# Five projection tiles summed block by block instead of four, with a sixth pair of split weight halves and a fourth adaLN buffer

## The chip, the cores and the metric

The kernel is one launch on one core of one Trainium2 chip. The metric is the device time of that launch in microseconds, the median of several runs. TensorE (PE) does the matrix products, VectorE (DVE) and ScalarE (ACT) the element-wise work, GpSimd (POOL) some sums and the small DMAs, and SyncE (SP) issues the large loads.

## What is computed

The trunk has two layers, and each layer is FFN, token mixer, FFN. That gives six sub-layers, numbered 0 to 5 here. Sub-layer 1 is the even mixer (windowed attention beside an RG-LRU), sub-layer 4 the odd mixer (HGRN2). There are 288 token columns: one prompt of 256 tokens and eight sequences of four. The width is 1024, kept as eight blocks of 128 rows. Each sub-layer is wrapped in the same way:

```python
def _pre(x, c, g_pre, ada_w, ada_b):
    mod = jax.nn.silu(c) @ ada_w + ada_b
    shift, scale, gate = jnp.split(mod[:, None, :], 3, axis=-1)
    return _rms_norm(x, g_pre) * (1 + scale) + shift, gate

def _post(x, y, gate, g_post, res_w):
    return x + res_w * (1 + gate) * _rms_norm(y, g_post)

def _swiglu(h, w_in, w_out):
    g, u = jnp.split(h @ w_in, 2, axis=-1)
    return (jax.nn.silu(g) * u) @ w_out
```

`h` is what `_pre` returns; the mixers too begin with a projection of `h` and end with a projection to `y`.

## The kernel before, in words

**Products.** Everything is kept transposed, features on partitions and 288 tokens in a row. A weight block W times h is three products of rounded halves: W_hi·h_hi, W_lo·h_hi and W_hi·h_lo. One output tile (128 features) of an input projection is `pj`, 8 blocks of h by 3 products, 24 matmuls. The output projection makes eight tiles `y0` to `y7` of 24 matmuls or more.

**Weights.** A load of 1 MB brings the weights of two `pj` tiles into one of `RAW` = 2 buffers `raw`; for each tile ACT rounds 128x1024 of it to `whi`, and DVE subtracts to get `wlo`. There are `HL` = 5 pairs of such halves. `split_some` issues the next split between matmuls when a pair is free in the plan.

**Order.** PE and SP run in the order in which the Python code emits. For ACT, DVE and POOL the framework sets an order when the program is built; it does not change at run time, so an instruction that waits holds up all that follows it on its engine. A planner (`clk`, `until`, `fill`, `ada_pace`, `drive`, `side`) keeps estimated times of all engines and decides between which matmuls the side work is emitted.

**From y to the next h (a transition).** After the last `y` tile the sums of squares (`yms`, `xyms`) are formed on PE, DVE and ACT make from them the two normalisers, which PE spreads (`yivb`, `xivb`), and then DVE and ACT make h block by block: `h0` high half, `h0` low half, `h1` and so on. `proj_in` meets these blocks with several tiles at once:

```python
for k in range(NB):
    group(range(outer), k)   # per tile 2 products with h_hi, then one with h_lo
...
for j in range(outer, n):    # the other tiles, one at a time
    w = get_w()
```

This first stretch is called the block phase here. `outer` is `OUTER` = 4, and it takes one weight pair for each of its tiles.

**adaLN.** The `mod` of every sub-layer comes from twelve chunks `ada` (two groups: eight of shift and scale, four of the gate), 64 chunks of 1 MB after the first eight, through `AW` = 3 buffers `aw`; SP issues each load when PE has read the buffer. After a group ACT copies it (`asb`), PE transposes it (`adaT`), and DVE writes `mod`. The planner uses a chunk, whole or in halves, to fill an expected wait of PE (`until`, `fill`), and otherwise spreads them (`ada_pace`). Where no chunk is at hand it may put a short `warm` product.

**Even mixer, end.** Its 14 tiles feed the recurrence (tiles 0 to 3), rotary and attention (4 to 9) and a gelu gate (10 to 13, `gx`). Attention runs as side work in four parts; scores of the eight short sequences are `scs`, their softmax `sms`, transposes `pT` and `pTs2`, products `pv1`, `pv0`, `pvs`. The gelu is done in `gated()`, which the last tile and the softmax of the short sequences both call: the one that is emitted second does it, with two loads of an activation table and the split of the gated result (`m`).

**Odd mixer, end.** For each of four pairs of heads a tree of products (`lv`, `sn`) runs beside the projection, with DVE and POOL updating Q, K and `acc` between its levels. Then come `ktp`, `sm`, `o`, the sum of squares `oms`, a normalisation on DVE and ACT, and the halves `o` of the pair, of which the output projection's `y0` needs all eight, in order; `o6` and `o7` are the last pair's.

Of the kernel before, what the change touches and what calls it, by code (L numbers as in the profile page):

```python
# [27 lines left out]
EPS = 1e-6  # L28
NEG = -1e30
NSUB = 6  # L30
RAW, HL, AW = 2, 5, 3
OUTER, KO = 4, 8
EV = 7.0
CV = (0.5, 1.5)
WARM = (28, 10, 4, 8, 8)
# [14 lines left out]
def tile_trunk(ctx: ExitStack, tc: tile.TileContext, I: dict, O: dict):  # L50
    nc = tc.nc
# [98 lines left out]
    def aux_ps(name):  # L150
        return ps.tile([128, 512], F32, tag="ps", name=name, bufs=8)

# [1 line left out]
    cT = cp.tile([128, NB, 32], F32, name="cT")  # L154
    SY.dma_start(cT, I["cT"].rearrange("p (k m) -> p k m", k=NB))
    sm = cp.tile([128, N_SMALL], F32, name="sm")
# [81 lines left out]
    sc = cT  # L238
    act(sc, cT, AF.Silu)

# [1 line left out]
    sides = []  # L242

    def dma_eta(nbytes, free=0.0):
# [25 lines left out]
    def until(*aps, gap=GAP, step=None):  # L270
        while ready(*aps) > clk["t"] + gap and (step or ada_ready()):
            if ada_ready():
                (step or ada_next)()
                run_sides()
            elif ready(*aps) > clk["t"] + KEEP:
                warm(1)
            else:
                break
# [15 lines left out]
            ada_next()  # L294
        clk["t"] = max(clk["t"], t)

# [1 line left out]
    units = []  # L298
    for i in range(NSUB):
        if i % 3 != 1:  # L300
# [31 lines left out]
    def get_w(load=True):  # L332
        q = oldest[0] = wat[0]
        wat[0] += 1
        split_to(q)
        if load:
            load_to(q // 2 + RAW)
        return splits[q]
# [7 lines left out]
    def mm3(out, w, o, hk, first, last):  # L346
        wh, wl = w[0][:, o:o + 128], w[1][:, o:o + 128]
        T.matmul(out, lhsT=wh, rhs=hk[:, 0, :], start=first, stop=False)
        T.matmul(out, lhsT=wh, rhs=hk[:, 1, :], start=False, stop=False)
        T.matmul(out, lhsT=wl, rhs=hk[:, 0, :], start=False, stop=last)  # L350

    def proj_in(n, hk, done, first=None):
        outer = OUTER
        ws = [get_w(False) for _ in range(outer)]
        oldest[0] = wat[0] - outer if not first else 0
        rest[0] = SPARE
        pp = [aux_ps(f"pj{j}")[:, :NT] for j in range(outer)]

        def group(js, k):
            o = 128 * k  # L360
            until(hk[k], gap=GAP if k else GAPS[4], step=ada_half)
            for j in js:
                T.matmul(pp[j], lhsT=ws[j][0][:, o:o + 128], rhs=hk[k][:, 0, :], start=k == 0, stop=False)
                T.matmul(pp[j], lhsT=ws[j][1][:, o:o + 128], rhs=hk[k][:, 0, :], start=False, stop=False)
            if first:
                first.finish(k)
            for j in js:
                T.matmul(pp[j], lhsT=ws[j][0][:, o:o + 128], rhs=hk[k][:, 1, :], start=False, stop=k == NB - 1)

        for k in range(NB):  # L370
            if first:
                first(k)
            group(range(outer), k)
            yield
        for j in range(outer):
            done(j, pp[j])
        for j in range(outer, n):
            w = get_w()
            p = aux_ps(f"pj{j}")[:, :NT]
            until(*w)  # L380
            for k in range(NB):
                mm3(p, w, 128 * k, hk[k], k == 0, k == NB - 1)
                yield
            done(j, p)
# [18 lines left out]
        A.activation(hk[:, 0, :], src, AF.Copy)  # L403
        V.tensor_tensor(out=hk[:, 1, :], in0=src, in1=hk[:, 0, :].bitcast(F32), op=OP.subtract)

# [1 line left out]
    mods = {}  # L407
    chunks = [(i, c) for i in range(NSUB) for c in range(NCH)]
    aw = []
# [107 lines left out]
            run_sides()  # L517
        drain()

# [1 line left out]
    def table(f):  # L521
        act(small("tab", [128, 1]), eps, f)

# [344 lines left out]
            side(x_stats(da.last))  # L868
        return hk

# [1 line left out]
    def ffn(hk, first=None):  # L872
        g2 = []
        st = {}

        def done(j, p):
            if j % 2 == 0:
                s = tmp("fs")
                act(s, p, AF.Silu)
                st["s"] = s  # L880
            else:
                m = st["s"]
                V.tensor_tensor(out=m, in0=m, in1=p, op=OP.mult)
                t = dbl(f"mh{j}", F32R)
                split_x(m, t)
                g2.append(t)

        drive(proj_in(2 * FB, hk, done, first))
        table(AF.Abs_reciprocal_sqrt)
        return g2  # L890

# [1 line left out]
    sp8 = cp.tile([128, 4], F32, name="sp8")  # L893
    sp16 = cp.tile([128, 4], F32, name="sp16")

# [68 lines left out]
    def even_mixer(hk):  # L964
# [194 lines left out]
        def done(j, p):  # L1159
# [17 lines left out]
            else:  # L1177
                b = j - 10
                A.activation(gxd[b // 2][:, b % 2, :], p, AF.Copy)
                if b == 3:  # L1180
                    gated()

        drive(proj_in(14, hk, done))
        drain()
        table(AF.Abs_reciprocal_sqrt)
        return mix

# [1 line left out]
    lb = cp.tile([128, 8], F32, name="lb")  # L1189
    oml = cp.tile([128, 8], F32, name="oml")  # L1190

# [183 lines left out]
    def odd_mixer(hk):  # L1375
# [39 lines left out]
        def gated(q, g, out):  # L1415
# [4 lines left out]
            split_x(o, out)  # L1420

        drive(proj_in(32, hk, done))
        drain()
        table(AF.Abs_reciprocal_sqrt)
        return mix

# [1 line left out]
    hk = None  # L1428
    for i in range(NSUB):
        first = None  # L1430
        if i == 0:
            hk, first = pre_first()
# [5 lines left out]
        mixer = i % 3 == 1  # L1438
# [10 lines left out]
def _prepare(a):  # L1449
# [37 lines left out]
    order = np.concatenate([np.arange(1280, 1792), np.arange(512, 768), heads, np.arange(768, 1280)])  # L1487
# [30 lines left out]
    r["rgw"] = g.transpose(1, 0, 2).reshape(128, 1024)  # L1518
    r["s0"] = a["state_s_hgrn"][0].transpose(1, 2, 0, 3).reshape(8, 128, 1024)

    # constants that depend on shapes alone
    r["ident"] = np.eye(128, dtype=f32)
    pos = np.concatenate([np.arange(NPR), np.tile(2048 + np.arange(TS), NSQ)]).astype(f32)
    inv = (f32(500000.0) ** (-np.arange(0, 16, 2, dtype=f32) / f32(16))).astype(f32)
# [72 lines left out]
```

## Time and profile before

| | before |
|---|---|
| median of 3 runs | 1321.88 us (1320.97 to 1321.97) |
| span of the profiled execution | 1320.2 us |
| PE busy | 1273.2 us, 96% |
| DVE, ACT, POOL busy | 61%, 47%, 17% |
| PE matmuls `pj` (with whi and with wlo) | 726.0 us and 519.0 us (they overlap in the records) |
| moved by DMA | 263.47 MB, 200 GB/s on average |

Matmuls overlap in the records, so busy PE time can be longer than the work; what a matmul costs is read from how many start in a stretch. The granted clock is 1.00 at 2.4 GHz and 0.50 at 1.2 GHz.

### The profile page before, as it was taken

How to read it: one execution, taken by the hardware profiler on the slowest of the kernel's cores; microseconds unless marked ns; L12 is line 12 of the kernel's file. 1: busy time of each engine (PE TensorE's matmuls, PEld its weight loads, DVE VectorE, ACT ScalarE, POOL GpSimd, SP SyncE). 2: the span in 40 equal slices, each digit the busy share in tenths (PEclk: the TensorE clock that was granted, in tenths of full speed). 3: DMA queues.
4: the chain of work that ended last, by engine and by line, in shares of the span. 5: the costliest groups of instructions: out<-in, count | busy, mean ns of one | idle time of the engine just before them, and what ended most of it. 6: DMA issues, size and time to landing. Idle time of an engine off the chain costs nothing. (4 is left out here: it accounts for less than half of the span.)

```text
span 1320.2 us, 25119 instructions
## 1 busy us (share of the span) xinstructions
PE 1273.2 (96%) x10267; PEld 1175.4 (89%) x10267; DVE 803.9 (61%) x1559; ACT 622.3 (47%) x1081; POOL 225.3 (17%) x303
## 2 busy tenths in 40 slices
PE   9999999999988999999899999989999989999995
PEld 7999999877687999999799999978788989999995
DVE  7644445688667555455754445488788777555433
ACT  5534444456654444444544444453445655444441
POOL 0000003263034000011400001153343132000011
PEclk9999999999999999999999999999999999999998
DMA  9786557466527745443675555367544452544441
GB/s 365 262 316 247 200 223 251 166 265 253 201 89 287 286 164 173 174 161 119 242 285 196 191 193 190 124 251 291 222 156 149 137 187 72 205 171 160 159 160 37
DMA packets 39556, 263.47 MB, mean 200 GB/s; under 512 B 4932, under 2 KB 5764, under 8 KB 9360
## 3 DMA queue, kind: packets, MB, share of 16 engines
q1 hardware_dynamic: 35280, 249.09, 51.6%
q0 software_dynamic: 4160, 12.77, 3.0%
q8 instruction: 81, 1.33, 0.4%
q14 instruction: 35, 0.29, 0.1%
HBM read 254.69 MB, written 7.15 MB: 198 GB/s over the span
## 5 line engine op out<-in xcount | busy, mean ns | idle before, releaser
L93 PE MATMUL pj<-h,whi 128*128 128x288 f32 x3552 | 726.0, 299 | 11.1 <-DVE h L93 8.6
L93 PEld LDWEIGHTS pj<-h,whi 128*128 128x128 f32 x3552 | 570.7, 189 | 45.9 <-issue 22.1
L93 DVE TENSOR_TENSOR wlo<-raw,whi 128x1024 fp32r<-128x1024 f32 x326 | 400.3, 1238 | 290.2 <-ACT whi L93 289.8
L93 PE MATMUL pj<-h,wlo 128*128 128x288 f32 x1776 | 519.0, 295 | 0.5 <-DVE wlo L93 0.5
L93 ACT ACTIVATE whi<-raw 128x1024 fp32r<-128x1024 f32 x326 | 340.4, 1058 | 341.4 <-PE pj L93 152.7
L93 PEld LDWEIGHTS pj<-h,wlo 128*128 128x128 f32 x1776 | 336.1, 189 | 0.7 <-DVE wlo L93 0.7
L93 PE MATMUL y<-mh,whi 128*128 128x288 f32 x1408 | 280.9, 295 | 0.0
L93 PEld LDWEIGHTS y<-mh,whi 128*128 128x128 f32 x1408 | 225.9, 188 | 2.9 <-issue 2.5
L93 PE MATMUL y<-mh,wlo 128*128 128x288 f32 x704 | 207.9, 295 | 0.0
L93 POOL TENSOR_TENSOR yss<-yss,ysq 128x288 f32<-128x288 f32 x55 | 59.5, 1082 | 789.4 <-ACT ysq L93 788.1
L93 PEld LDWEIGHTS y<-mh,wlo 128*128 128x128 f32 x704 | 132.4, 188 | 0.0
L93 DVE TENSOR_TENSOR fs<-fs,pj 128x288 f32<-128x288 f32 x88 | 39.5, 453 | 98.2 <-PE pj L93 90.9
L93 PE MATMUL ada<-aw,cT 128*32 128x512 f32 (+1 forms) x656 | 67.8, 515 | 0.0
L93 ACT ACTIVATE mh<-fs 128x288 fp32r<-128x288 f32 x88 | 37.7, 433 | 59.5 <-DVE fs L93 59.5
L93 ACT ACTIVATE fs<-pj 128x288 f32<-128x288 f32 x88 | 34.8, 400 | 37.1 <-PE pj L93 37.0
L93 ACT ACTIVATE h<-hn,mod 128x256 fp32r<-128x256 f32 x48 | 24.4, 509 | 56.1 <-DVE hn L93 56.1
L93 POOL TENSOR_TENSOR yg<-yg,yivs 128x288 f32<-128x288 f32 x38 | 34.0, 905 | 91.5 <-ACT yivs L93 91.5
L93 DVE TENSOR_TENSOR mh<-fs,mh 128x288 fp32r<-128x288 f32 x88 | 39.5, 453 | 11.2 <-ACT mh L93 11.2
L93 ACT ACT_TABLE_LOAD x27 | 34.6, 1283 | 16.2 <-PE pj L93 9.5
L93 PE MATMUL y<-o,whi 128*128 128x288 f32 x192 | 40.0, 302 | 0.5 <-DVE o L93 0.5
L93 ACT ACTIVATE ysq<-y 128x288 f32<-128x288 f32 x42 | 17.0, 404 | 44.1 <-PE y L93 44.1
L93 PEld LDWEIGHTS y<-o,whi 128*128 128x128 f32 x192 | 31.7, 193 | 1.8 <-ACT o L93 0.8
(289 smaller groups left out, 1086.9 us busy)
## 6 DMA issues: line engine op xcount, KB each, us to landing
raw<-in_wf_in SPq DMA_DIRECT2D x88, 1024.0 KB, 4.9
aw<-in_w_ada SPq DMA_DIRECT2D x64, 1024.0 KB, 5.0
raw<-in_wf_out SPq DMA_DIRECT2D x44, 1024.0 KB, 4.9
raw<-in_wo_in SPq DMA_DIRECT2D x16, 1024.0 KB, 6.9
awf<-in_w_ada SPq DMA_DIRECT2D x8, 1024.0 KB, 9.2
raw<-in_we_in SPq DMA_DIRECT2D x7, 1024.0 KB, 6.9
raw<-in_we_out SPq DMA_DIRECT2D x4, 1024.0 KB, 7.8
S<-in_s POOLq DMA_DIRECT2D x16, 256.0 KB, 7.3
```

The costliest lines, as they stand in the source:

```text
L93: r = f(*args, **kw)
```

## The change

`HL` goes from 5 to 6, `AW` from 3 to 4 and `OUTER` from 4 to 5; the first sub-layer keeps four tiles in its block phase. The room comes from `dynamic_dma_scratch_size=2048`, which makes the scratch of POOL's DMAs smaller: 2,048 bytes a partition instead of 16,384 in the built program. Six comment lines are left out too, without effect.

```diff
-RAW, HL, AW = 2, 5, 3
-OUTER, KO = 4, 8
+RAW, HL, AW = 2, 6, 4
+OUTER, KO = 5, 8
...
     def proj_in(n, hk, done, first=None):
-        outer = OUTER
+        outer = 4 if first else OUTER
...
-    nc = _bacc.Bacc("TRN2", target_bir_lowering=False, num_devices=1)
+    nc = _bacc.Bacc("TRN2", target_bir_lowering=False, num_devices=1, dynamic_dma_scratch_size=2048)
```

The planner answers the new buffers with another order everywhere. The products are the same, and there are four `warm` products and two loads of an activation table fewer (27 to 25). From the end of the even mixer on the adaLN chunks run earlier. At the end of the even mixer eight chunks stand between the last `pj` and `y0` instead of three. In the four later transitions fewer chunks stand before the second h block: three instead of four after sub-layers 0, 2 and 3, none instead of one after sub-layer 4, where a following transpose `adaT` also stood. In the odd mixer one chunk is left of eleven, and none stands in its `y0`. On SP, nine adaLN loads now go ahead of the last four weight loads of the even mixer's output projection.

Three places show what moved. The first is ACT at the end of the even mixer, from the second softmax of the short sequences (`sms`) on; `gx` is the gelu, `m` the gated result, `pTs` the copy that releases `pv0`. Before:

```order
L93 ACTIVATE sms,den<-sms,mx 128x288
L93 ACTIVATE es<-es 128x1
L93 ACTIVATE o_3913<-pv_3562 128x128
L93 ACT_TABLE_LOAD
L93 ACTIVATE gx_3030<-gx_3030 128x2x288
L93 ACTIVATE o_3916<-pv_3562 128x128
L93 ACTIVATE pTs<-pT 128x512
L93 ACTIVATE gx_3031<-pj_3884 128x288
L93 ACTIVATE m_3948<-ob 128x288
L93 ACTIVATE gx_3031<-gx_3031 128x2x288
```

Now:

```order
L93 ACTIVATE sms,den<-sms,mx 128x288
L93 ACTIVATE es<-es 128x1
L93 ACT_TABLE_LOAD
L93 ACTIVATE gx_3034<-gx_3034 128x2x288
L93 ACTIVATE gx_3035<-gx_3035 128x2x288
L93 ACT_TABLE_LOAD
L93 ACTIVATE tab<-eps 128x1
L93 ACTIVATE m_3949<-ob 128x288
L93 ACTIVATE m_3955<-ob 128x288
L93 ACTIVATE m_3961<-ob 128x288
L93 ACTIVATE m_3967<-ob 128x288
L93 ACTIVATE pTs<-pT 128x512 x2
```

Both copies `pTs` for `pv0` now stand behind the whole gelu; before, the first stood ahead of `sms` and the second in the middle of the gelu. PE meanwhile has, after `scs`, one set of four `pT` and two chunks ahead of `pv0`.

The second is PE at the end of the odd mixer, around the last pair of heads (`pj_11749` is the last projection tile, `y_11826` is `y0`). Before, from the products `o` on, with projection matmuls on both sides of them:

```order
L93 MATMUL pj_11701<-h_9410,wlo 128x288
L93 MATMUL pj_11749<-h_9403,whi 128x288 x2
L93 MATMUL pj_11749<-h_9403,wlo 128x288
L93 MATMUL o<-acc,vt 128x128 x2
L93 MATMUL o<-acc,vt 128x32
L93 MATMUL o<-sel,Xs 128x32
L93 MATMUL o<-Q_10981,smid 128x128
L93 MATMUL o<-acc,vt 128x128 x2
L93 MATMUL o<-acc,vt 128x32
L93 MATMUL o<-sel,Xs 128x32
L93 MATMUL o<-Q_10981,smid 128x128
L93 MATMUL pj_11749<-h_9404,whi 128x288 x2
```

Before, further on, inside `y0` ahead of `o6`:

```order
L93 MATMUL y_11826<-o_11695,whi 128x288 x2
L93 MATMUL y_11826<-o_11695,wlo 128x288
L93 MATMUL ada_11851<-aw_8_10095,cT 32x512 x4
L93 MATMUL ada_11851<-aw_9_10263,cT 32x512 x4
L93 MATMUL ada_11851<-aw_10_10408,cT 32x512 x4
L93 MATMUL y_11826<-o_11748,whi 128x288 x2
```

Now, from the end of the last projection tile to `y0`:

```order
L93 MATMUL pj_11710<-h_9472,wlo 128x288
L93 MATMUL ktp<-ident,K_10804 128x128 x4
L93 MATMUL sm<-vt,kt 128x128 x4
L93 MATMUL o<-acc,vt 128x128 x2
L93 MATMUL o<-acc,vt 128x32
L93 MATMUL o<-sel,Xs 128x32
L93 MATMUL o<-Q_10805,smid 128x128
L93 MATMUL o<-acc,vt 128x128 x2
L93 MATMUL o<-acc,vt 128x32
L93 MATMUL o<-sel,Xs 128x32
L93 MATMUL oms<-osq,ones 128x288 x2
L93 MATMUL y_11840<-o_11288,whi 128x288 x2
```

The projection matmuls that stood between the steps of the last pair, 21 between `ktp` and `sm`, 6 between `o` and `oms` and 15 after `oms`, are done before it, and the three chunks in `y0` are gone.

The third is DVE at the first transition, after the last `y` of sub-layer 0 (`nt` is the first step of the normaliser). Before:

```order
L93 SCALAR_TENSOR_TENSOR ysq_2821<-y_2717,modG_144,x 128x256
L93 TENSOR_TENSOR yg_2712<-y_2717,modG_144 128x32
L93 TENSOR_TENSOR ysq_2821<-x,yg_2712 128x32
L93 TENSOR_TENSOR ysq_2822<-yg_2712 128x32
L93 SCALAR_TENSOR_TENSOR nt<-yms,yiv 128x72
```

Now:

```order
L93 SCALAR_TENSOR_TENSOR ysq_2836<-y_2695,modG_144,x 128x256
L93 TENSOR_TENSOR yg_2690<-y_2695,modG_144 128x32
L93 TENSOR_TENSOR ysq_2836<-x,yg_2690 128x32
L93 TENSOR_TENSOR ysq_2837<-yg_2690 128x32
L93 TENSOR_TENSOR wlo<-raw,whi 128x1024
L93 SCALAR_TENSOR_TENSOR nt<-yms,yiv 128x72
```

A weight split stands between the squares and the normaliser there; its `whi` stands on ACT just ahead of `yiv`.

## Rows read from the trace of the kernel before

**Rows 1.** The page: costliest groups (busy us, mean ns, idle before, its main releaser).

```profile
L93 PE MATMUL pj<-h,whi 128*128 128x288 f32 x3552 | 726.0, 299 | 11.1 <-DVE h L93 8.6
...
L93 DVE TENSOR_TENSOR wlo<-raw,whi 128x1024 fp32r<-128x1024 f32 x326 | 400.3, 1238 | 290.2 <-ACT whi L93 289.8
...
L93 ACT ACTIVATE whi<-raw 128x1024 fp32r<-128x1024 f32 x326 | 340.4, 1058 | 341.4 <-PE pj L93 152.7
```

**Rows 2.** Timeline of PE after sub-layer 0 (start us, us; idle before and releaser).

```profile
265.97 1.07 PE L93 MATMUL ada<-aw,cT 128*32 128x256 f32 x16
...
270.36 0.96 PE L93 MATMUL adaT<-sm,asb 128*128 128x18 f32 x8
...
273.72 0.93 PE L93 MATMUL pj<-h,whi 128*128 128x288 f32 x5 [1.26 <-DVE h L93]
```

**Rows 3.** Stretches: length, busy time of PE, PEld, DVE, ACT, POOL, PEclk, DMA.

```profile
357.50:360.00 2.50, 2.31 (x19) 2.10 (x19) 0.00 (x0) 0.16 (x2) 0.00 (x0) 0.61 1.01 426
360.00:365.00 5.00, 5.00 (x22) 5.00 (x23) 0.77 (x4) 0.77 (x4) 0.00 (x0) 0.51 0.97 405
365.00:370.00 5.00, 5.00 (x40) 5.00 (x39) 0.65 (x2) 2.44 (x5) 0.72 (x1) 1.00 0.02 7
...
637.50:641.50 4.00, 3.90 (x18) 3.90 (x19) 4.00 (x17) 2.27 (x8) 0.75 (x1) 0.57 0.98 410
...
872.40:874.00 1.60, 1.52 (x8) 1.52 (x9) 1.60 (x7) 0.82 (x3) 1.24 (x2) 0.67 0.97 410
...
1085.00:1092.00 7.00, 5.13 (x19) 4.29 (x19) 5.91 (x16) 2.08 (x7) 4.81 (x6) 0.51 0.00 1
```

**Rows 4.** Timeline of PE after sub-layer 4, in the block phase.

```profile
1097.29 0.93 PE L93 MATMUL pj<-h,whi 128*128 128x288 f32 x5 [1.24 <-DVE h L93]
```

**Rows 5.** Timeline of PE at the end of the even mixer.

```profile
342.31 0.41 PE L93 MATMUL scs<-kv,qs 64*128 64x32 f32 x2
...
355.13 0.43 PE L93 MATMUL pvs<-pTss,vt 32*64 32x128 f32 x2 [1.06 <-ACT pTss L93]
...
357.69 0.43 PE L93 MATMUL pvs<-pTss,vt 32*64 32x128 f32 x2 [0.62 <-ACT pTss L93]
```

**Rows 6.** Timeline of ACT at the end of the even mixer.

```profile
347.09 0.53 ACT L93 ACTIVATE sms<-sms,mx 128x288 f32<-128x288 f32 x1 [0.43 <-DVE mx L93]
...
347.99 1.28 ACT L93 ACT_TABLE_LOAD   x1
349.28 0.68 ACT L93 ACTIVATE gx<-gx 128x576 f32<-128x576 f32 x1
...
350.03 0.59 ACT L93 ACTIVATE pTs<-pT 128x512 f32<-128x512 f32 x1
...
353.74 0.76 ACT L93 ACTIVATE m<-ob 128x288 fp32r<-128x288 f32 x2
```

**Rows 7.** Timeline of all engines at the end of sub-layer 1.

```profile
385.14 1.06 ACT L93 ACTIVATE whi<-raw 128x1024 fp32r<-128x1024 f32 x1 [2.65 <-DMA raw<-in_wf_in]
...
388.16 0.33 PE L93 MATMUL yms<-yss,ones 128*32 128x72 f32 x8 [1.21 <-POOL yss L93]
...
389.33 0.33 PE L93 MATMUL yms<-ysq,ones 128*32 128x72 f32 x8 [0.83 <-ACT ysq L93]
...
391.18 0.46 PE L93 MATMUL xyms<-ysq,ones 128*32 128x72 f32 x16 [1.26 <-DVE ysq L93]
```

**Rows 8.** Timeline of DVE after sub-layer 1, between the normaliser and x.

```profile
399.79 0.82 DVE L93 SCALAR_TENSOR_TENSOR modG<-mod,gph 128x72 f32<-128x72 f32 x1
```

**Rows 9.** Timeline of PE in the odd mixer, and of its end.

```profile
931.86 0.51 PE L93 MATMUL oms<-osq,ones 128*128 128x288 f32 x1 [1.42 <-ACT osq L93]
...
1048.00 1.13 PE L93 MATMUL oms<-osq,ones 128*128 128x288 f32 x4
...
1057.03 0.40 PE L93 MATMUL y<-o,whi 128*128 128x288 f32 x1 [0.50 <-DVE o L93]
```

**Rows 10.** Ten stretches of 20 us from 860 us: their sum over the odd mixer.

```profile
sum 200.00, PE 194.23 PEld 165.86 DVE 163.09 ACT 97.08 POOL 76.26; mean PE 19.42 PEld 16.59 DVE 16.31 ACT 9.71 POOL 7.63
```

## The prediction

> **What bounds the kernel now.** I began with the page. TensorE (PE) runs almost without a break, so the time is its work plus its idle time plus what it loses where its clock is granted at the lower level. The other engines matter only where PE waits for them. The costliest group tells of the largest single cause: PE stands 11.1 us ahead of `pj` matmuls, 8.6 of it for DVE's half of `h` [rows 1]. That is the block phase, at which the change aims. Then I read the timeline of PE at each transition and at the end of both mixers, and the granted clock of those stretches. In the first later transition the reader sees where chunks hide PE's waits, that a chunk costs 1.0 us and an `adaT` 0.8 us from start to start, and that the last wait, 1.26 us, is for the low half of `h1` on DVE [rows 2]. From the next block on PE no longer waits, with four tiles already. So a fifth tile helps only by what it puts ahead of that wait: three matmuls of `h0` and two of `h1`. A matmul takes 0.13 us at the full clock (40 records in 5 us) and 0.23 at half (22 in 5 us) [rows 3]. **Five matmuls are 0.66 us a transition**, not the whole wait, and a chunk that leaves this place takes back 1.0.
>
> **The change part by part.** All terms are PE time, against the profiled span of 1320.2 us.
>
> *After sub-layer 0.* 0.66 us more of `pj`, 1.0 us less of chunks: +0.3. The new `wlo` ahead of `nt` takes 1.24 us on DVE, on the chain that ends in `h1`; its `whi` of 1.06 us on ACT lies beside it and ahead of `yiv`, which would have waited for the sums about half of that [rows 1]. Behind it wait `nt`, both normalisers, all of `h`, and PE. +1.6 in all, between +0.5 (the split slips into an idle stretch of DVE) and +2.
>
> *End of the even mixer.* Before, PE waited here 1.06 and 0.62 us [rows 5] and then ran at half clock: (1 - 0.61) x 2.5 + (1 - 0.51) x 5.0 = 3.4 us lost [rows 3]. Together 5.1 us, which eight chunks instead of three might remove. But `pv0` now waits for a `pTs` behind the whole gelu on ACT, and the gelu stands behind `sms`, which needs `scs`. From the end of `scs` (342.72) [rows 5] to the second `sms` were 4.4 us, through DVE [rows 6]. Then come `sms` and `es` 0.6, a table load 1.28, two `gx` of 0.6, a second load 1.28, `tab` 0.1, four `m` of 0.38, one `pTs` of 0.6: 11.0 us [rows 6]. PE has four `pT` and two chunks for that time, 2.6 us. The wait is 8.4 us if the 4.4 stand, and 7.1 if the one `wlo` of 1.24 us [rows 1] inside them finds room elsewhere; I take 7.5. A wait of that length will be followed by half clock, as the stretch of 0.51 after sub-layer 4 was [rows 3]; part of such a stretch passes within the wait, so between 0 and 3.4 us are lost, and I take 1.0. Sum: 7.5 + 1.0 - 5.1 = **+3.4**, between +2.0 and +6.7.
>
> The table loads in this sum are weighed on ACT's rows: the gelu starts 1.29 us after its load starts, so a load costs 1.28 and no more [rows 6]. The Trainium skill (page "ScalarE: Activation LUTs", section "What ACT_TABLE_LOAD costs") gives 2.66 us for each switch, the load of 1283 ns and a drain of 1380 ns. By it the two switches would add 2.8 us and the sum would end at 1330.4 instead of 1327.6; the row shows the load alone, so I use that.
>
> *Transition after sub-layer 1.* Before, ACT stood 2.65 us for a weight load, and the sums behind it made PE wait 1.21, 0.83 and 1.26 us [rows 7]. The new order has most of these splits earlier; the nine adaLN loads ahead on SP delay four weight loads, but these are due only for the last tiles of `y` and for the next sub-layer. I keep 0.4 of the 3.3: -2.9. `modG`, 0.82 us [rows 8], and the small `mod` beside it leave the chain: -1.0. Five tiles: -0.7, with as many chunks as before. **-4.6**, between -5 and -1, the latter if a load is late again.
>
> *After sub-layers 2 and 3.* One chunk and the `adaT` leave, 1.8 us, and 0.7 comes: +1.1 each. Against it the half clock inside their block phases goes: (1 - 0.57) x 4.0 = 1.7 after sub-layer 2, and (1 - 0.67) x 1.6 = 0.5 behind the last wait after sub-layer 3 [rows 3]. With no chunk ahead of `xivb` the clock will fall earlier instead, as after sub-layer 4; that slows `yivb` and `xivb` on the chain, 0.3 us each by the doubled pace. Sum +1.2, between -1 and +3.
>
> *After sub-layer 4.* No chunk and no `adaT` are left, 0.7 of `pj` comes, and the wait that ended at 1097.29 with 1.24 us [rows 4] grows: +1.1, between 0 and +2.
>
> *Odd mixer, inside.* The wait of 1.42 us ahead of `oms` [rows 9] came from ACT behind a weight load that stood behind an adaLN load on SP; with ten chunks fewer there it goes: -1.4, at worst 0.
>
> *Odd mixer, end.* Before, projection matmuls and three chunks lay beside the last pair's steps, and PE waited 0.50 us [rows 9]. Now nothing does. ACT's copies of `ktp` leave 0.7 us ahead of `sm`, the square of the second `o` 0.7 ahead of its `oms`. From the end of `oms` (1049.13) to the last half of `o` were 7.9 us [rows 9], with two table loads that are gone from there: 7.9 - 2.6 = 5.3. The first 18 matmuls of `y0` cover 2.4 of it, so 2.9 remain. 4.3 us instead of 0.5, and 0.6 for the clock: **+4.4**, between +2.5 and +6.5.
>
> *At nothing.* The sixth pair and fourth buffer are what the order above uses. `warm` products lie in waits. The smaller scratch for POOL's DMAs appears in no row; POOL is idle four fifths of the time and PE waits for none of its issues, so I take 0, with -0.5 and +3 as ends, the upper being some late loads of state in the odd mixer at the price of the load-caused waits seen [rows 7].
>
> **Sum:** 1.6 + 3.4 - 4.6 + 1.2 + 1.1 - 1.4 + 4.4 = +5.7 us of waits and clock; the work itself is unchanged, since a chunk costs the same wherever it stands. That gives a span of 1325.9 us. The median before lies 1.7 us above the profiled span, so I forecast **1327.6 us**.
>
> **The rivals.** *The phase waits vanish (faster).* If the fifth tile covered all 8.6 us for which `pj` waits for DVE's `h` [rows 1], instead of 0.66 at each of five transitions, the terms of the transitions other than the chain terms become -8.6; with +1.3 for the split after sub-layer 0, -1.0 and -2.9 after sub-layer 1, and the mixers as above (+3.4, -1.4, +4.4) that is -4.8: 1317.1 us. For it speaks the row; against it that the wait comes ahead of the second block, where only five matmuls are new, and that chunks have been taken from that place. It decides at 1.26 us of `pj` ahead of the wait.
>
> *Gains and losses cancel (no change).* If DVE and ACT reach `sms` and the last pair's steps sooner than PE, both ends cost half, 3.9 us less: 1323.7 us. For it: both engines are idle more than a third of the time. Against: both chains begin at a PE instruction (`scs`, the last `lv`), so they cannot start ahead of it.
>
> *The tree of the odd mixer becomes the bound (much slower).* DVE is busy 163.09 of 200 us there [rows 10]. PE gets ten chunks less, 10 us, in that stretch, while DVE's work stays. If the chain of DVE steps between the `lv` levels holds its time, PE waits at the `lv` of the last two pairs for up to 10 us less what is already counted at the end (4.4), 5.6 more: 1333.2 us. For it: DVE has the least room there of all engines but PE. Against: PE waited at no `lv` before, and the new order puts more `pj` between the levels. It decides where DVE's idle time, 18% before and 14% in a stretch of 190 us, no longer takes up the waits between the levels.
>
> *The clock.* That the granted clock falls after a wait of PE is in this trace: 0.51 from 1085 us on, in the transition after sub-layer 4, where no chunk hides PE's waits for the normalisers [rows 3]. The Trainium skill (page "TensorE: Matmul & The Clock Gate", section "HAM oscillation — how this bites in real kernels") says that idle stretches bring the lower clock back each time, and it speaks against a change that moves fillers out of waits. If each of the two long waits were followed by a full stretch at half clock, that would be 2.4 us more after `pv0` and some 1.2 more at the end of the odd mixer: 1331.2 us, inside the range.
>
> **How the numbers follow.** About 0.2%, 2.6 us, is what a measurement of this kernel can tell from no change: 1319.2 to 1324.5. Forecast, slower, 1324.5 to 1331: 0.47. Tree or lower clock beyond that: 0.14. Cancelling: 0.21. Phase waits vanish: 0.18. So faster 0.18, same 0.21, slower 0.61. The range leaves out a tenth on either side: low 1317.5, near the first rival's time, high 1335.0, the tree's time and part of the clock's.
>
> **What would show it.** In the profile after: one PE wait of 7 us ahead of `pv0`, released by ACT `pTs`, with PEclk near 0.5 around it; waits of together about 4 us between the last `pj` of the odd mixer and `y1`; no ACT wait for a weight load before the end of sub-layer 1; a wait ahead of `h1` at every later transition, longer after sub-layer 4. I am wrong if `pv0` starts without a wait, if the waits for `h` fall well below 8.6 us in sum, or if PE waits at `lv`.

## The result, and the profile after

| | before | after |
|---|---|---|
| median | 1321.43 us (1320.29 to 1321.97) | 1349.08 us (1348.35 to 1351.06) |
| span of the profiled execution | 1320.2 us | 1347.2 us |
| mean granted clock of TensorE | 0.987 | 0.976 |

The change makes the kernel slower: ratio 1.022, interval 1.0204 to 1.0236. The direction was forecast (1327.6 us), the size was not: the profiled span rose by 27.0 us instead of 5.7, and the time lies above the upper end, 1335.0.

The page after, the groups of [rows 1] (busy us, mean ns, idle before, its main releaser):

```profile
L93 PE MATMUL pj<-h,whi 128*128 128x288 f32 x3552 | 722.9, 298 | 4.5 <-DVE h L93 3.5
...
L93 DVE TENSOR_TENSOR wlo<-raw,whi 128x1024 fp32r<-128x1024 f32 x326 | 400.1, 1242 | 241.4 <-ACT whi L93 240.1
L93 PE MATMUL pj<-h,wlo 128*128 128x288 f32 x1776 | 517.6, 295 | 2.3 <-DVE wlo L93 2.2
```

The five tiles do what the change says: PE's wait for DVE's `h` falls from 8.6 us to 3.5 in all. What came instead is in PE's waits after (us in total, times, longest):

```profile
PE pv L93 <- ACT pTs L93: 7.9, 1, 7.9
PE xivb L93 <- DVE rt L93: 7.6, 6, 2.2
...
PE adaT L93 <- ACT asb L93: 3.3, 2, 2.8
PE y L93 <- ACT o L93: 3.3, 1, 3.3
PE xyms L93 <- ACT ysq L93: 3.3, 1, 3.3
...
PE vtp L93 <- ACT vs L93: 1.4, 1, 1.4
```

To see where the time went I cut both timelines of PE at the same matmuls and took from each piece its matmuls `pj` and `y` (0.132 us each) and its adaLN work at full clock: the chunks (0.12 us for 512 columns, 0.06 for 256) and `adaT`. What is left is waits, lower clock and small products. The forecast is put to the piece in which each of its terms lies: of the 3.4 us of half clock at the end of the even mixer that were to go, 2.4 lie behind the first matmul of `y0`, which starts at 359.87 us in the kernel before. Difference, after less before:

| piece | forecast | measured |
|---|---|---|
| after sub-layer 0: chain to the first `pj` / block phase | +1.6 | +8.6 / -2.1 |
| even mixer up to `y0` | +5.8 | +7.5 |
| `y` of sub-layer 1 and transition after it | -7.0 | -3.9 |
| FFN of sub-layers 2 and 3, behind the block phase | 0 | +2.9, +5.3 |
| after sub-layers 2 and 3: chains / block phases | +1.2 | +3.6, +4.6 / -3.3, -3.3 |
| odd mixer up to `y0` | 0.0 | +2.5 |
| odd mixer, inside `y` | +3.0 | +5.1 |
| after sub-layer 4, and the rest | +1.1 | +0.5 |
| sum | +5.7 | +28.0 |

The span rose by 27.0. Single pieces are good to about 0.3 us, since they depend on the rates and on the matmul at which a piece is cut.

**After sub-layer 0.** Timeline of PE, ACT, DVE and POOL there, in that order, and then stretches of this place (columns as in [rows 3]):

```profile
264.97 0.33 PE L93 MATMUL xyms<-ysq,ones 128*32 128x72 f32 x8 [3.29 <-ACT ysq L93]
267.00 1.30 PE L93 MATMUL yivb<-diag,hot 128*128 128x288 f32 x2 [1.70 <-DVE diag L93]
...
263.29 1.06 ACT L93 ACTIVATE whi<-raw 128x1024 fp32r<-128x1024 f32 x1 [3.32 <-DMA raw<-in_we_in]
...
270.47 3.66 DVE L93 TENSOR_TENSOR x<-x,yg 128x288 f32<-128x288 f32 x1
...
270.19 0.57 POOL L993 DMA_DIRECT2D out_v_old<-vc  x1
270.77 0.80 POOL L93 TENSOR_TENSOR x<-x,yg 128x288 f32<-128x288 f32 x1
271.52 2.29 POOL L93 TENSOR_TENSOR yg<-yg,yivs 128x288 f32<-128x288 f32 x3
```

```profile
260.00:265.00 5.00, 1.35 (x36) 0.83 (x37) 1.50 (x5) 1.71 (x4) 0.00 (x0) 1.00 1.02 426
265.00:270.00 5.00, 3.30 (x26) 1.23 (x26) 3.90 (x16) 1.99 (x7) 0.55 (x1) 0.55 0.98 413
270.00:275.70 5.70, 4.94 (x28) 2.45 (x24) 5.63 (x8) 0.44 (x2) 5.53 (x9) 0.50 0.92 316
```

The split that the new order puts into the chain finds no weights yet: ACT stands 3.32 us for the load. The squares behind it come late, PE stands 3.29, and from 265 us on the clock is the lower one. Then DVE's first add of x takes 3.66 us; in the kernel before, the same add took 1.05 (at 264.49).

**End of the even mixer.** PE, ACT and stretches; these answer to [rows 5], [rows 6] and [rows 3]:

```profile
365.47 1.97 PE L93 MATMUL pv<-pTs,vt 128*64 128x512 f32 x2 [7.89 <-ACT pTs L93]
...
359.54 1.28 ACT L93 ACT_TABLE_LOAD   x1
360.83 1.26 ACT L93 ACTIVATE gx<-gx 128x576 f32<-128x576 f32 x2
362.11 1.28 ACT L93 ACT_TABLE_LOAD   x1
...
364.84 0.57 ACT L93 ACTIVATE pTs<-pT 128x512 f32<-128x512 f32 x1
```

```profile
360.00:365.00 5.00, 0.00 (x0) 0.00 (x0) 3.28 (x12) 4.96 (x10) 0.00 (x0) 0.61 0.79 301
365.00:371.50 6.50, 6.03 (x16) 1.50 (x16) 0.53 (x2) 1.50 (x3) 0.00 (x0) 0.51 0.12 25
```

**The sums of sub-layer 1.** PE, ACT and DVE there; these answer to [rows 7]:

```profile
405.19 0.33 PE L93 MATMUL yms<-ysq,ones 128*32 128x72 f32 x8 [0.47 <-ACT ysq L93]
...
407.53 0.46 PE L93 MATMUL xyms<-ysq,ones 128*32 128x72 f32 x16 [1.76 <-DVE ysq L93]
...
405.82 1.06 ACT L93 ACTIVATE whi<-raw 128x1024 fp32r<-128x1024 f32 x1 [0.32 <-DMA raw<-in_wf_in]
...
403.93 2.89 DVE L93 TENSOR_TENSOR wlo<-raw,whi 128x1024 fp32r<-128x1024 f32 x2
```

ACT's wait for the weights is down to 0.32 us, but two splits stand on DVE ahead of the last square, and PE still waits 2.2 us for the sums.

**FFN and odd mixer.** Waits of PE that the kernel before has not, or has shorter (`vtp` 0.61 us, `y` 0.50), at these places:

```profile
513.91 0.40 PE L93 MATMUL pj<-h,wlo 128*128 128x288 f32 x1 [1.49 <-DVE wlo L93]
...
685.39 1.89 PE L93 MATMUL adaT<-sm,asb 128*128 128x18 f32 x8 [2.84 <-ACT asb L93]
...
921.38 0.55 PE L93 MATMUL vtp<-ident,vs 128*128 128x128 f32 x3 [1.41 <-ACT vs L93]
...
1083.64 0.90 PE L93 MATMUL y<-o,whi 128*128 128x288 f32 x2 [3.31 <-ACT o L93]
```

### The profile page after: what moved, and what is told of

Read it like the earlier page. It is cut to its first block, busy times and chain, and to the rows that moved or that the text cites. A ratio compares the mean times of both kernels' runs of the same rounds, so it can differ in the third digit from the quotient of the medians.

```text
span 1347.2 us, 24963 instructions
## 1 busy us (share of the span) xinstructions
PE 1284.3 (95%) x10227; PEld 1177.1 (87%) x10227; DVE 803.5 (60%) x1559; ACT 616.9 (46%) x1079; POOL 224.7 (17%) x303
## 4 chain that ended last, share of the span: by engine, by line
PE 84%; DVE 9%; ACT 3%; issue 2%; DMA 1%; POOL 0%; DVEq 0%; SPq 0%; ACTq 0%
PE pj L93 50%; PE y L93 24%; PE ada L93 3%; DVE wlo L93 2%; PE lv L93 1%; DVE x L93 1%; DVE hs L93 1%; ACT whi L93 1%; PE o L93 1%; DMA raw<-in_we_in 1%; PE adaT L93 1%; PE pv L93 1%; DVE xc L93 1%; PE adaf L93 1%; DVE rt L93 0%
## 5 line engine op out<-in xcount | busy, mean ns | idle before, releaser
L93 PE MATMUL ada<-aw,cT 128*32 128x512 f32 (+1 forms) x624 | 72.1, 581 | 0.8 <-DMA aw<-in_w_ada 0.8
L93 PEld LDWEIGHTS ada<-aw,cT 128*32 128x32 f32 x624 | 17.5, 121 | 27.1 <-issue 24.3
```

The costliest lines, as they stand in the source:

```text
L93: r = f(*args, **kw)
```

## The experiments

Each kernel is told of by what the planner counts with (tiles, pairs, adaLN buffers: 4/5/3 before, 5/6/4 after) and what is really there.

### One part at a time

```diff
 e1:  RAW, HL, AW = 2, 5, 4    OUTER = 4
 e2:  RAW, HL, AW = 2, 6, 3    OUTER = 5
 e3:  RAW, HL, AW = 2, 6, 3    OUTER = 4
 e4:  RAW, HL, AW = 2, 5, 3    OUTER = 4
 (all with dynamic_dma_scratch_size=2048)
```

> The kernel before with a fourth adaLN buffer (and the smaller scratch), four tiles, five pairs. Theory A (the fourth buffer carries the loss: its loads go ahead of weight loads on SP, and its chunks are used up outside the waits): 1338 to 1350 us. Theory B (the loss sits in a few places of the new order, and this order has one of them, the gelu ahead of pv0, and only two and a half chunks after sub-layers 2 and 3, but no weight split in the chain after sub-layer 0 and projection work beside the last pair of the odd mixer): about +6 for pv0, +2 to +4 for the two transitions, 1329 to 1333 us. Theory C (the fifth tile and sixth pair carry it): 1321 to 1324 us.

> The changed kernel with three adaLN buffers: five tiles, six pairs, smaller scratch. Its order has the split in the chain after sub-layer 0, four chunks in the transitions after sub-layers 0 to 3, and chunks between the last pair's steps at the end of the odd mixer. Theory A: 1315 to 1322 us (the loss goes with the buffer, the gain of the fifth tile stays). Theory B: the split +6 to +9, five transitions -0.7 to -3 each, 1321 to 1327 us. Theory C: 1340 us or more.

> The kernel before with a sixth pair of split halves (and the smaller scratch), four tiles, three adaLN buffers. Its order has the split between the squares and the normaliser after sub-layer 0, as the changed kernel; the other places are near to before. Theory B: +6 to +9 us there, 1327 to 1331 us, with an ACT wait for a weight load of some 3 us at that place. Theory A: 1320 to 1323 us, since with three buffers SP does not hold adaLN loads ahead of that weight load, and the split costs at most its own 1.2 us.

> Only the smaller scratch of POOL's DMAs; four tiles, five pairs, three adaLN buffers as before, and every engine's order as before. If the scratch has no part in it: 1321.4 us, within 0.2%. If POOL's DMAs suffer by it (rival): slower, up to the whole 27 us of the change, with loads of state that land later than the 7.3 us before.

Measured, against 1320.07 us: scratch alone 1319.16 (0.9993, interval 0.9976 to 1.0010); fourth adaLN buffer alone 1336.91 (1.0126, 1.0108 to 1.0144); sixth pair alone 1345.22 (1.0188, 1.0164 to 1.0212); five tiles and sixth pair 1353.68 (1.0255, 1.0229 to 1.0281). So the small scratch costs nothing, as forecast, and neither buffer carries the loss alone: each, added by itself, makes the kernel slower, and one of them with 25 us nearly as much as the whole change. The two don't add up either (17 + 25 against 27). None of the three theories held throughout: e1 fell between the ranges of A and B, e2 into that of C, and e3 lies 14 us above B's. The traces differ from each other at the same places: the chain after sub-layer 0 holds the split whenever six pairs are counted, and the gelu stands ahead of `pv0` in e1 too. The sixth pair alone, ACT after sub-layer 0:

```profile
263.03 1.06 ACT L93 ACTIVATE whi<-raw 128x1024 fp32r<-128x1024 f32 x1 [2.23 <-DMA raw<-in_we_in]
```

That a buffer costs time speaks for the order that the planner writes with it. The next runs hold the order and change the buffers.

### The order of before with the buffers of after

```diff
 RAW, HL, AW = 2, 5, 3          # the planner's numbers, as before
-hi = wp.tile(..., name="whi", bufs=HL)
-lo = wp.tile(..., name="wlo", bufs=HL)
+hi = wp.tile(..., name="whi", bufs=6)
+lo = wp.tile(..., name="wlo", bufs=6)
-w = wp.tile(..., name=f"aw{i}_{c}", bufs=AW)
+w = wp.tile(..., name=f"aw{i}_{c}", bufs=4)     # e7; e11 keeps AW = 3 here
```

The orders of PE and SP are then those of before; on ACT, DVE and POOL the framework sets another order, mostly with splits earlier.

> Four tiles and TensorE's instruction order exactly that of before (the planner counts with 5 pairs and 3 adaLN buffers), but 6 split pairs, 4 adaLN buffers and the 2048 byte descriptor area of after are there, so splits and loads may run earlier. Theory order (the buffers cost nothing; what costs is the instruction order that the planner writes when it counts with them): 1316 to 1323, ratio within 0.3% of before, and none of the waits of 3.3 us ahead of the yiv sum after sub-layer 0 or of 7.9 us ahead of pv0. Rival buffers (earlier splits and loads come in the way of ScalarE's urgent work, or the loads of each other): near the sum of e1 and e3, 1340 or more.

> Four tiles, TensorE's and the queue's order of before, 6 pairs, 3 adaLN buffers. The run with both buffers gained 7 us. Theory pair (the late weight load at the end of sub-layer 1 and the half clock behind it went because a split can start earlier): 1311 to 1315. Rival adaLN buffer (its loads start earlier and leave the DMA engines to the weights): 1317 to 1321.

Measured: both buffers **1312.66 us** (1309.71 to 1313.04) against 1319.23, ratio 0.9944, interval 0.9929 to 0.9959: **faster than before, by 0.6%, and so than after**; 3 us below the range of my theory. The sixth pair alone 1316.64 against 1318.80, 0.9981 (0.9966 to 0.9996): about a third of the gain; the rest comes with the fourth adaLN buffer, so that neither theory of e11 holds by itself. The largest single piece of the gain is the `y` of sub-layer 1 (3.6 us of 8.7 by the cuts above). There ACT's wait of 2.65 us for a weight load [rows 7] becomes 0.70, and PE's waits for the sums of 1.21, 0.83 and 1.26 us become 0.22 and 0.33. ACT and PE with both buffers:

```profile
379.61 1.07 ACT L93 ACTIVATE whi<-raw 128x1024 fp32r<-128x1024 f32 x1 [0.70 <-DMA raw<-in_wf_in]
...
386.93 0.33 PE L93 MATMUL yms<-ysq,ones 128*32 128x72 f32 x8 [0.22 <-ACT ysq L93]
...
387.74 0.33 PE L93 MATMUL xyms<-yss,ones 128*32 128x72 f32 x8 [0.33 <-POOL yss L93]
```

By the medians the buffers gain 6.6 us. The loss of the change is in the order.

### Four tiles in the planner's new order

```diff
 RAW, HL, AW = 2, 6, 4
-OUTER, KO = 5, 8
+OUTER, KO = 4, 8
```

> Four tiles; the planner counts with 6 pairs and 4 adaLN buffers, which are there. Theory order (the planner's order, not the number of tiles, makes the loss): split in the chain after sub-layer 0 (+8), gelu ahead of pv0 (+5 to +10), so 1335 to 1347. Rival tiles (five first tiles make the loss of after): 1311 to 1322, as the four tile run with these buffers in the old order.

Measured 1346.10 us (1344.90 to 1351.86), ratio 1.0204, interval 1.0175 to 1.0233, which holds the 1.022 of after. With the same buffers counted, four tiles and five can't be told apart by the time. The places differ, though: by the cuts above e5 loses nothing in the chains after sub-layers 2 and 3 and under 1 us in their FFN, but 15 us in the even mixer. So the near equality is of two different orders, and shows of the fifth tile only that its gain in the block phases doesn't appear in the whole.

### Five tiles without a sixth pair in the plan

```diff
 e6:   RAW, HL, AW = 2, 5, 3   OUTER = 5
 e10:  the same, but bufs=6 for whi and wlo, bufs=4 for aw, as in e7
```

> Five tiles with the 5 pairs and 3 adaLN buffers of before. The order has no weight split in the chain after sub-layer 0, but gelu ahead of both pTs copies and the last adaLN chunks of the odd mixer ahead of its output. Theory order: even mixer +7 to +10 as in after, odd mixer +3 to +6, transitions with the split's 6.5 gone, blocks of h -2 each: 1326 to 1336. Rival pairs (five first tiles need six pairs, since the five hold all pairs and the next split waits for the first to come free): waits ahead of the sixth tile of 1 to 3 us at each of five sub-layers, 1340 or more.

> Five tiles; the planner counts with 5 pairs and 3 adaLN buffers as in the five tile run with these, but 6 pairs and 4 adaLN buffers are really there. Theory order (five tiles make no time of themselves; the waits of 10 to 13 us ahead of the sixth tile's weights go with the sixth pair, the order with gelu ahead of pv0 and the odd mixer's late tail stays): block phases fall by 73 us against the run with 5 pairs, 1330 to 1345. Rival tiles (the five tiles gain the 2 to 3 us a sub-layer that the waits for h were worth once the buffers are there): below the 1312.7 of the four tile run with these buffers.

Measured 1417.80 us (1.0756, 1.0723 to 1.0790) and 1410.72 (1.0684, 1.0664 to 1.0705), far outside my theories: e6 lost over 80 us more than its theory allowed. Of the rivals of e6 the one of the pairs had the kind of wait right, but not its size, 9 to 13 us instead of 1 to 3. The waits of PE in e6 name the reason, and the timelines of PE and ACT in e10 its place:

```profile
PE pj L93 <- ACT whi L93: 61.3, 6, 12.7
```

```profile
280.62 0.61 PE L93 MATMUL pj<-h,whi 128*128 128x288 f32 x1 [11.62 <-ACT whi L93]
...
279.41 0.21 ACT L93 ACTIVATE h<-hs 128x32 fp32r<-128x32 f32 x1
279.53 1.04 ACT L93 ACTIVATE whi<-raw 128x1024 fp32r<-128x1024 f32 x1
```

Once a transition has been emitted, the code holds every later split behind its last `h` (`after(a, clk["prior"][0])`). With five pairs counted, the fifth tile's split is one of these. Buffers that are there without being counted help little, as e10 shows. Five tiles therefore need a split ahead of or within each chain. The sixth pair in the plan allows that, and the `whi` after sub-layer 0 is the price.

### The split after sub-layer 0

```diff
 def split_some(steps):
     rest[0] -= steps
+    if clk.get("late"):
+        return
 e8:   late() sets clk["late"] = True;    e12:  clk["late"] = b == NB - 1 at each y tile
+clk["late"] = False     # both, at the end of the transition
```

> After, with no weight half split by the planner between the start of a sub-layer's closing sums and the end of its transition; the halves come by the next projection instead. Theory (the 3.3 us that ScalarE waits for the late load with a split in the chain after sub-layer 0, and the half clock after it, cost 6.5): 1341 to 1345, chain after sub-layer 0 as short as in e1 (net 4 to 5 us, not 13.4), full clock in it. Rival: the load is as late for the next projection, which then waits for the weights at its first tiles: within 2 of after, 1347 to 1351.

> After, with no weight half split by the planner from the last y tile on until the end of the transition; in the run before with the same aim the split in question was queued ahead of that point and stayed. Here it is out of the chain after sub-layer 0. Theory (that split costs 6.5 there): chain after sub-layer 0 at net 4 to 5.5 instead of 13.4, full clock in it, and 1338 to 1343 in all; the splits of the chains after sub-layers 2 and 3 go as well, worth 0 to 1 each. Rival (the next projection waits for the weights instead): 1346 to 1351, with waits for weights of 3 us or more in the block of h.

e8 measured 1350.75 us (1.0240, 1.0222 to 1.0257), as after; but this says nothing about the theory, since the split was emitted ahead of `late()` and stayed on ACT with a wait of 3.02 us. e12 took it out and lost: 1411.50 us (1.0691, 1.0668 to 1.0715). The wait moved into the block phase as in e10, 9.02 us, already ahead of the fourth tile, and 9 to 11 us at each of the four later ones. My rival had the place right, but its time lay 60 us too low. The edit holds back the splits of all five transitions, so it doesn't price the one after sub-layer 0 by itself. It does show that with five tiles the splits can't all wait for the end of the chain; what is left to try is that the load comes sooner.

### Why the load was late, and the long add

```diff
 e13:
+clk["dg"] = dg.last          # POOL's last add of the transition
-G.dma_start(O["k_old"]..., kcv...)
+after(G.dma_start(O["k_old"]..., kcv...), clk["dg"])      # and the same for v_old
 e14:
-ada_load_to(n + AW)
+if not clk.get("late"): ada_load_to(n + AW)      # late: from y7 to the end of the transition
 e15:  both
```

> After, with GpSimd's four issues of the old key and value outputs kept behind GpSimd's last add of the transition after sub-layer 0; TensorE's order is that of after. In after one of these issues (0.57 us) stands between GpSimd's first product and its first add, and VectorE's first x add beside it takes 3.66 us instead of the 1.05 of before. Theory (the issue makes GpSimd's five following operations run through without a gap, and VectorE's add only ends behind them): that add near 1.05, chain 2 to 3 shorter, 1344.5 to 1347. Rival (the add is long because the chain before it was late, not for the issue): the add stays near 3.6, within 1 us of after.

> After, with the adaLN loads that come free from the last y tile on issued only at the end of the transition, so that the late weight load after sub-layer 0 has the DMA engines to itself. Theory (that load takes 11 us because four adaLN loads run beside it; without them it lands before the closing sums and ScalarE's 3.3 us wait goes): ScalarE's wait ahead of that weight half under 1 us, no wait of 3.3 us ahead of the xyms sums, 1338 to 1344. Rival (fewer adaLN tiles are there to fill the transitions, the planner shifts them, and what is won is lost there): 1345 to 1352.

> Both edits, the held adaLN loads and the outputs behind the chain. Theory (the loss after sub-layer 0 is the late load's wait of 3.3, the add's 2.6 and the half clock they bring): chain after sub-layer 0 at net 4.5 to 6.5 as in before, 1336 to 1342. Rival (one cause alone holds the chain, or the planner's later order eats it): not faster than the better of the two by more than 1.

Measured against 1321.73 us: e13 **1342.57** (1.0161, 1.0145 to 1.0177), e14 1343.62 (1.0165, 1.0146 to 1.0184), e15 1339.95 (1.0139, 1.0115 to 1.0163). e13, with the order of PE as in after, gains more than its theory gave: its profiled span is 7.7 us shorter than that of after. Of this 4.8 us lie in the chain after sub-layer 0, where it cures both ills. DVE, ACT and the clock in e13:

```profile
266.60 1.05 DVE L93 TENSOR_TENSOR x<-x,yg 128x288 f32<-128x288 f32 x1
...
259.83 1.05 ACT L93 ACTIVATE whi<-raw 128x1024 fp32r<-128x1024 f32 x1
```

```profile
265.00:271.50 6.50, 5.37 (x33) 2.74 (x26) 6.25 (x14) 2.09 (x6) 5.76 (x7) 0.50 0.98 382
```

The add is back at 1.05 us, and ACT no longer waits for the weights. The transfers from 246 to 264 us say why (issues, KB each, median us from issue to landing), first of after, then of e13:

```profile
q0 software_dynamic: 560, 1.81, 36.4%
...
raw<-in_we_in SPq DMA_DIRECT2D x1, 1024.0 KB, 11.0
```

```profile
q0 software_dynamic: 320, 1.05, 17.7%
...
raw<-in_we_in SPq DMA_DIRECT2D x1, 1024.0 KB, 6.8
```

Without POOL's old keys and values the same load, issued at the same time, lands 4.2 us sooner. The chain after sub-layer 0 falls from 16.6 us to 11.8, with the same chunks in it. So the outputs beside it made the load slow; adaLN loads run beside it in both. e14 shows that it was also issued late. On SP it stood behind an adaLN load; with that held back it is issued at 245.18 us instead of 252.23, and ACT's wait for it was 1.18 us and over long before the sums. That adaLN loads beside it make it slow, as the theory of e14 has it, was not tested by this. In e14 the add still took 3.67 us, PE waited 3.38 for the first `h`, and only 1.0 us of chunks was left in the chain, of 2.9. e15 has both edits: add 1.04 us, chain 10.5 with 1.0 us of chunks (before: 8.9 with 3.8). Its interval overlaps that of e13, so that the second cure on top isn't shown to bring anything. In e13 the clock in this chain is still the lower one, behind a wait of 1.70 us for `diag` that stayed.

### The gelu ahead of `pv0`

```diff
-gated()                       # when emitted second, at once
+side(gelu_after())            # waits for both pTs copies of the last part, then gated()
```

> After, with the gelu group (two table loads, two gelu, four products) queued on ScalarE behind both pTs copies of the last attention instead of ahead of them. Theory (the 7.9 us wait at pv0 is the place of gelu in the queue and with the half clock after it costs what the even mixer lost): wait at pv0 under 2 us, 1339 to 1344. Rival: the gelu's results are then late for the first y tile instead, the wait moves there: 1346 to 1350.

Measured 1346.57 us (1342.69 to 1352.84), ratio 1.0210, interval 1.0179 to 1.0241. The profiled span is 3.1 us shorter than that of after, and by the cuts above the even mixer lost 3.6 us instead of 7.5, but the runs don't separate the two. PE there:

```profile
357.54 1.07 PE L93 MATMUL pv<-pTs,vt 128*64 128x512 f32 x2 [0.29 <-ACT pTs L93]
...
360.59 1.07 PE L93 MATMUL pv<-pTs,vt 128*64 128x512 f32 x2 [0.40 <-ACT pTs L93]
...
366.89 1.07 PE L93 MATMUL adaT<-sm,asb 128*128 128x18 f32 x8 [2.90 <-ACT asb L93]
```

```profile
368.00:378.50 10.50, 10.50 (x61) 7.85 (x62) 1.42 (x7) 1.32 (x6) 0.00 (x0) 0.51 0.72 287
```

The wait of 7.9 us is the gelu's place: moved, it is 0.7. But the copy `asb` now stands behind the gelu, PE waits 2.90 us for that, and the work that follows runs at the lower clock. Both theories were half right: the wait fell as the first said, and a good part of the gain went into a new wait as the second said, though at `adaT` and not at the first `y` tile.

## Why the prediction was right or wrong

**What bounds the kernel.** Right that PE's waits and clock are the time; and the page shows the mark that I had set against myself: the waits for `h` fell to 3.5 us. The step "five matmuls are 0.66 us a transition" was too small: the waits for DVE's `h` in the block phases fell by 2.1 us after sub-layer 0, 1.7 after 2 and 1.4 after 3, and rose by 0.9 after 1. I had priced only the last wait of each phase, and there are two. It hardly mattered, because the chains ahead of them lost more.

**After sub-layer 0** (+1.6 forecast, +6.5 measured). The step that failed is the price of the split: I took DVE's 1.24 us and let `whi` lie "beside it". I did not ask when its weights land. ACT stood 3.32 us for them; e14 shows that the load was issued late, behind an adaLN load, and e13 that POOL's outputs then delayed it. These were moved by the change: in before the last of them is issued at 252.71 us, ahead of the chain, in after one falls into it (270.19), where the add beside it took 2.6 us more. My part "At nothing" looked at POOL's queue only for the small scratch and not for the order of its DMAs. The lower clock came on top.

**End of the even mixer** (+5.8 up to `y0`, +7.5). The mechanism and the wait were right: 7.89 us, released by `pTs` behind the gelu, against 7.5. The term that failed is the clock behind it. I took 1.0 us of 0 to 3.4; the stretch from 365 to 371.5 us shows 0.51 with PE at work for 6.03 of the 6.5 us, (1 - 0.51) x 6.0 = 2.9, close to the upper bound. e9 shows that the place of the gelu makes the wait, and also that its removal alone isn't measurable.

**After sub-layer 1** (-7.0 from `y0` on, -3.9). The half clock in `y0` went, as forecast, and that is the greater part of the gain: 22 matmuls in the 5 us from 360 us on [rows 3] are worth 2.9 us at full clock, so 2.1 were lost there. The step that failed is "I keep 0.4 of the 3.3": ACT's wait for the weight load fell from 2.65 us to 0.32, but PE waits 0.47 and 1.76 us for the sums, 2.2 in all, since two `wlo` on DVE (2.89 us) stand ahead of the last square. The 0.7 us for five tiles did not come either: the waits for `h` on DVE and ACT together are 2.3 us there, against 2.6 before. That the measured -3.9 looks like the -4.6 of this term is luck.

**FFN of sub-layers 2 and 3** (0, +8.2). This had no step. I had compared orders at transitions and mixers and took the long middle of an FFN to be PE's alone. But a chunk group ends in `asb`, and ACT has other things ahead of it: after sub-layer 3's block phase a table load, `fs`, four splits and `mh`, so PE stood 2.84 us at `adaT`, and the clock fell: 0.50 from 685.4 to 691.6 us, with PE at work throughout, (1 - 0.50) x 6.2 = 3.1. In sub-layer 2 it was 1.49 us for a `wlo` and 0.50 at an `adaT`, and the clock stayed.

**After sub-layers 2 and 3** (+1.2, +1.6). The sum was right by luck, with two wrong terms in it: the block phases gained 3.3 each, where the forecast has 2.4 and 1.2 (five tiles and the half clock that goes), and the chains lost 3.6 and 4.6 instead of 1.8 of filler and 0.6 of clock. In the chain after sub-layer 2 the clock is the lower one throughout. The same chain in after and, below it, in before:

```profile
651.20:658.00 6.80, 5.26 (x30) 2.81 (x34) 5.79 (x17) 1.82 (x6) 3.88 (x5) 0.50 0.01 4
```

```profile
624.00:631.00 7.00, 5.12 (x70) 2.78 (x62) 6.41 (x21) 2.69 (x10) 3.58 (x5) 1.00 0.87 317
```

**Odd mixer** (+3.0, +7.6). The end came as told: waits of PE of 4.5 us against 4.3, the longest 3.31 at `y0`. With it goes 1.15 at `sm` instead of 0.7, and none at `oms`. The clock behind them lost 1.7 and not 0.6: 0.72 from 1084 to 1090 us, (1 - 0.72) x 6.0. Inside, the wait ahead of `oms` went as forecast (-1.4), but 1.41 us at `vtp` (0.61 before) and 0.61 and 0.53 at `dg` came, all of them for copies on ACT. The tree did not become the bound: only 0.2 us of waits at `lv`. That this mixer lost in every order that the planner wrote anew (3.5 to 11 us in e1, e2, e3, e5, e6) was seen; which of the planner's decisions does it was not tried and stays open.

**After sub-layer 4.** The wait of 1.24 us ahead of the second block, which I had growing by 1.1, fell to 0.49.

**The rivals.** "The clock" named the right force and the wrong places: it looked only behind the two long waits. "The phase waits vanish" was half true of the phases. The largest error was one of scope, with the FFN alone at 8.2 us: of an order rewritten everywhere I priced the places that I had looked at and set the others to 0.

## What to carry to other kernels

When buffers feed a planner, more room is a new program: build the old order with the new buffers first (here -6.6 us), and only then let the order change (here the whole ended at +27, so the order took back some 34). Of each instruction that a new order puts into a chain, ask what it waits for and what runs beside that, the DMA issues on the quiet engine included. A step that gives PE more to do ahead of a wait moves that work away from the wait before it, so price the chain and its block together.

## What the runs showed of the hardware

**A VectorE add held by GpSimd.** The first 128x288 add `x<-x,yg` after sub-layer 0 took 3.66 to 3.70 us in the eight profiles in which a DMA issue of GpSimd stands between GpSimd's first product and its first add (after, e2, e3, e5, e8, e9, e12, e14), and 1.04 or 1.05 us in the nine in which none does (before, e1, e4, e6, e7, e10, e11, e13, e15). In after it begins at 270.47, 0.30 us ahead of GpSimd's add (in the other seven 0.30 or 0.31 too; in the nine GpSimd's add begins 0.15 or 0.16 us ahead of VectorE's); GpSimd's next four operations run from 270.77 to 273.81, and VectorE's add ends at 274.13. The Trainium skill (page "SBUF — State Buffer", section "Who interferes with whom") says that a VectorE instruction with two inputs in SBUF contends with a GpSimd instruction that reads SBUF, for ports that are an exclusive lock. The trace agrees: in after VectorE's add ends 0.32 us behind the last of the four. That it lost to four instructions in a row, though it had begun ahead of them, is what these profiles show beyond that. Moving the DMA issue away, in e13, moves the add back to 1.05 us; whether the issue itself decides it, or only which of the two adds begins first, these profiles can't tell, since the two go together in all seventeen.

**Small stores and a large load.** Three stores of 248 KB beside a 1 MB load went with 11.0 us to its landing instead of 6.8 (after and e13); both were issued at 252.2 us, with adaLN loads beside them.

**The clock in a chain of small products.** It was not only the wait of 7.9 us that brought the lower clock. In the chain after sub-layer 2 it came from 651.2 us on, and PE's waits ahead of that were 0.50, 0.27 and 0.78 us, between small products.
